# Gate tiles 4 and 5 of the second merge gate as a sixth pair by seven block products, and three convolution channels between the attention heads

## Chip, cores and metric

One core of a Trainium2 chip runs the whole program. The metric is device time in microseconds (us). The kernel before has a median of 817.81 us over 3 runs (817.81 to 818.59). Engines are named as in the profile: PE is the matmul engine, DVE the vector engine, ACT the scalar engine, POOL is GpSimd, and SP issues most of the loads.

## What is computed

The reference is one decoder layer on x of 512 tokens and 1024 channels, all in float32 (biases, gains and the second half are cut):

```python
u = _rmsnorm(h, norm1_g)
a_glu, q, k, v, r, g_low, gate_a, gate_b = _split_cols(u @ w_in)
c = a_glu[..., :CONV_CH] * jax.nn.sigmoid(a_glu[..., CONV_CH:])
c = _causal_dwconv(c, conv_dw_w, conv_dw_b)          # 31 taps over the tokens
y_conv = jax.nn.silu(_layernorm(c, ...)) @ w_conv_out
o = _gla_chunked(q, k, v, decay(g_low))               # 4 heads, chunks of 64 tokens
y_gla = (rmsnorm_by_head(o) * jax.nn.silu(r)) @ w_gla_out
merged = jax.nn.sigmoid(gate_a) * y_conv + jax.nn.sigmoid(gate_b) * y_gla
h = h + merged @ w_o
h = h + feed_forward(rmsnorm(h))
```

## The kernel before

**A tile of work.** Every projection is made in tiles of 128 output channels by 512 tokens; the 1024 input channels are eight blocks of 128. A float32 product is three matmuls in a rounded format (L529, L530, L531 in mm3): the weights and the activations are each split into a high part and a low rest, and the product of the two rests is left out. A plain tile is so 8 blocks by 3, 24 matmuls of 128x512. The names wlo and whi in the profile are the low and high part of a weight tile.

**Weights.** The list `order` (L244 to L274) fixes in which order weight tiles are loaded, split and used. ACT writes the high part (L414, L444), and the low part comes from one of three places: a subtraction on DVE (L415, L452), one on POOL (L450), or, for the tiles in the set ADDED, a negation on ACT (L446) and a DMA that adds the weights on top (L447). LOOK makes the split run two tiles ahead of its use. PE takes its weights strictly in that order, so a low part that comes late stops it.

**Seven products instead of eight.** Two kinds of work are done by a scheme of seven block products in place of eight on a 2 by 2 block matrix. In `seven` (L1440) w_r runs so, over all its tiles. In `two_tiles` (L1331) two gate tiles p and q are one pair: in four steps, x1, x3, x2 and x4, seven products of 128x256 matmuls, four input blocks by three each, which makes 84 matmuls. The sums of weights that a pair needs are made on POOL (L386), and the pair's results are put together by ACT copies (L1338) and DVE additions (L1341). The activations' own sums (L1293, L1306) are made once for w_r and all pairs. MERGE lists the pairs, `pair_7` (L1566) runs one of them, and BEHIND and PLAIN_GLA say which tiles of the w_gla and w_conv projections run inside a pair, by halves of four blocks, or behind it. Inside the first pair `pair_7` also runs `gated_o` (L1233), which transposes the gated head outputs on PE (L1237), two of them behind the last step of w_r already.

**The convolution.** Each of 8 channel tiles k has a gated unit (`glu`, L960), two weight tiles, from whose product the convolution's input comes. Its 31 taps are then worked off on the vector engines: `conv_chain` (L873) splits the tokens into even and odd, so that some 45 half-length taps do it. A tap is one DVE instruction (L889) of up to 255 elements, into the tiles called c and aside. A number of rows of taps per channel (ROWS) can go to POOL instead: ACT scales two tap inputs (L922) and one POOL addition of both halves (L924) stands for two DVE taps; `run_ahead` gives POOL these rows only while an earlier chain is being worked off, and those that it has not got to by then are DVE's. The list of one channel is the chain of that channel. `fill` (L505) hands out chain work by shares: each call of `weight` pays some work behind the DVE operation of the weight just split. The eight channels are then summed (L983, L986) for a normalization, whose statistics are spread on PE (L1014).

**The order of the stages.** w_v first half; channels 0 to 5 of the gated units; w_low; w_v second half; then a loop over the heads that overlaps queries and keys of one head (L1160 to L1173), and scores (L1188), states (L1199 to L1206) and outputs (L1217, L1219) of the head before; between these stand the late channels 6 and 7 (LATE_GLU, heads 1 and 2) and gate_b tiles 0 to 5 (AHEAD; heads 3 and the pass behind the last head); w_r; the five pairs with the w_gla tiles; w_conv; w_o; the feed-forward part. `pair_7(0)` works off every chain but the last of the list behind its third step (`while len(after) > 1`).

## Time and profile before

| what | value |
|---|---|
| time, median of 3 runs | 817.81 us |
| span of the profiled execution, first to last instruction | 816.3 us |
| median less span | 1.5 us |
| mean granted PE clock | 0.998 |
| w_low to the end of w_v | 98 to 124 us |
| heads and gate_b tiles | 124.6 to 246 us |
| w_r | 246 to 284.5 us |
| first pair, with two w_gla tiles behind it | 285.2 to 309.4 us |

The profiled execution has no time of its own beside its span; the 1.5 us are what lies around it, if it ran as the median did. The times of the stages are those of PE's rows in the trace. A row of the timeline gives start, duration, engine, line, operation, result and operands, a count where equal rows are joined, and in brackets the idle time of that engine before it with what ended it. A row of the windows gives for each engine the busy time in a stretch.

### The profile page before, as it was taken

What the parts mean: (1) busy time and instruction counts of PE and PEld (TensorE: products, weight loads), DVE (VectorE), ACT (ScalarE), POOL (GpSimd) and SP (SyncE); (2) the same over time, 40 slices, a digit from 0 to 9 for tenths busy, and PEclk for the clock granted to TensorE, in tenths of its full rate; (3) what the DMA queues carried; (4) which work ended last, traced back from release to release, by engine and by line L of the source; (5) the groups of instructions that cost most, each with busy time, mean ns of one, the idle gap of its engine ahead of it and who ended that gap; (6) DMA issues with size and microseconds to landing.
All of it is one profiled execution on the core that took longest, in us unless ns stands there. A gap on an engine that the chain in (4) does not pass through costs nothing.

```text
span 816.3 us, 11459 instructions
## 1 busy us (share of the span) xinstructions
PE 807.2 (99%) x4227; PEld 694.4 (85%) x4227; DVE 699.1 (86%) x1103; ACT 489.3 (60%) x749; POOL 192.6 (24%) x168
## 2 busy tenths in 40 slices
PE   9999999999999999999999999999999999999996
PEld 7888888888888898989888898898889987899885
DVE  6779999998998988486779899979976999789896
ACT  6667788677546665494535655556445663366555
POOL 2025433332204332122001100320123311622010
PEclk9999999999999999999999999999999999999999
DMA  9487758645831232432458513145732346224562
GB/s 338 143 196 181 189 160 177 160 116 133 189 97 58 80 128 78 142 108 89 166 136 217 176 64 118 52 155 155 160 120 82 142 116 167 104 104 173 163 129 104
DMA packets 36472, 113.60 MB, mean 139 GB/s; under 512 B 3688, under 2 KB 8944, under 8 KB 36416
## 3 DMA queue, kind: packets, MB, share of 16 engines
q1 hardware_dynamic: 28912, 86.39, 29.9%
q0 software_dynamic: 7488, 26.48, 18.1%
q8 instruction: 33, 0.54, 0.2%
q14 instruction: 23, 0.19, 0.1%
q10 hardware_dynamic: 16, 0.00, 0.0%
HBM read 110.76 MB, written 2.10 MB: 138 GB/s over the span
## 4 chain that ended last, share of the span: by engine, by line
PE 87%; DVE 11%; DMA 1%; issue 0%; ACT 0%; SPq 0%; ACTq 0%; DVEq 0%
PE mm L529 20%; PE mm L530 20%; PE mm L531 20%; DVE c L889 5%; PE cv L529 4%; PE cv L530 4%; PE cv L531 4%; DVE aside L889 3%; PE ax L531 2%; PE ax L530 2%; PE ax L529 2%; PE mm L743 2%; PE ax L1217 1%; PE cv L743 1%; PE ax L1219 1%; DMA raw<-in_w_v_dram 1%
## 5 line engine op out<-in xcount | busy, mean ns | idle before, releaser
L529 PE MATMUL mm<-uh,wlo 128*128 128x512 f32 (+1 forms) x532 | 194.2, 365 | 0.0
L530 PE MATMUL mm<-ul,whi 128*128 128x512 f32 (+1 forms) x532 | 191.9, 361 | 0.0
L531 PE MATMUL mm<-uh,whi 128*128 128x512 f32 (+1 forms) x532 | 191.7, 360 | 0.0
L415 DVE TENSOR_TENSOR wlo<-raw,whi 128x1024 fp32r<-128x1024 f32 x82 | 94.6, 1161 | 35.6 <-ACT whi L414 31.7
L386 POOL TENSOR_TENSOR raw<-raw,raw 128x512 f32<-128x512 f32 x39 | 61.8, 1585 | 235.6 <-DVE wlo L415 132.0
L529 PEld LDWEIGHTS mm<-uh,wlo 128*128 128x128 f32 x532 | 100.6, 189 | 15.2 <-DVE wlo L452 0.3
L531 PEld LDWEIGHTS mm<-uh,whi 128*128 128x128 f32 x532 | 100.5, 189 | 15.3
L530 PEld LDWEIGHTS mm<-ul,whi 128*128 128x128 f32 x532 | 100.6, 189 | 14.8
L414 ACT CAST whi<-raw 128x1024 fp32r<-128x1024 f32 x82 | 78.8, 965 | 40.0 <-PE mm L531 25.0
L444 ACT CAST whi<-raw 128x1024 fp32r<-128x1024 f32 x80 | 83.5, 1048 | 29.1 <-PE mm L531 13.9
L452 DVE TENSOR_TENSOR wlo<-raw,whi 128x1024 fp32r<-128x1024 f32 x50 | 66.0, 1326 | 7.2 <-ACT whi L444 7.0
L414 ACT CAST whi<-kept 128x1024 fp32r<-128x1024 f32 (+1 forms) x40 | 40.2, 1008 | 31.0 <-DVE kept L362 15.7
L415 DVE TENSOR_TENSOR wlo<-kept,whi 128x1024 fp32r<-128x1024 f32 (+1 forms) x40 | 47.4, 1186 | 6.4 <-ACT whi L414 6.4
L889 DVE SCALAR_TENSOR_TENSOR aside<-cv,pp,aside 128x255 f32<-128x255 f32 (+6 forms) x112 | 52.2, 466 | 0.0
L889 DVE SCALAR_TENSOR_TENSOR c<-aside,btmp,c 128x247 f32<-128x247 f32 (+13 forms) x93 | 52.0, 565 | 0.0
L889 DVE SCALAR_TENSOR_TENSOR c<-cv,pp,c 128x247 f32<-128x247 f32 (+13 forms) x93 | 43.3, 465 | 1.4 <-ACT c L885 1.4
L446 ACT ACTIVATE wlo<-raw 128x1024 fp32r<-128x1024 f32 x28 | 29.4, 1059 | 19.0 <-PE mm L529 19.0
L1338 ACT COPY tmp<-mm 128x256 f32<-128x256 f32 x38 | 14.1, 370 | 36.5 <-PE mm L531 35.8
L1720 DVE SCALAR_TENSOR_TENSOR tmp<-mm,pp,tmp 128x511 f32<-128x511 f32 (+1 forms) x42 | 31.2, 742 | 4.0 <-ACT tmp L1717 3.9
L1720 DVE SCALAR_TENSOR_TENSOR tmp<-tmp,pp,tmp 128x511 f32<-128x511 f32 (+1 forms) x32 | 27.8, 888 | 0.4
L1491 DVE TENSOR_TENSOR hres<-hres,mm 128x512 f32<-128x512 f32 (+1 forms) x37 | 24.6, 675 | 2.2 <-PE mm L531 2.1
L530 PE MATMUL cv<-ul,whi 128*128 128x512 f32 (+1 forms) x72 | 25.7, 356 | 0.0
(507 smaller groups left out, 2084.0 us busy)
## 6 DMA issues: line engine op xcount, KB each, us to landing
raw<-in_w_up_dram SPq DMA_DIRECT2D x44, 512.0 KB, 3.6
raw<-in_w_glu_dram SPq DMA_DIRECT2D x16, 512.0 KB, 5.7
raw<-in_w_down_dram SPq DMA_DIRECT2D x15, 512.0 KB, 3.3
wlo<-in_w_glu_dram POOLq DMA_DIRECT2D x12, 512.0 KB, 7.4
kept<-in_w_down_dram POOLq DMA_DIRECT2D x10, 512.0 KB, 5.5
raw<-in_w_v_dram SPq DMA_DIRECT2D x8, 512.0 KB, 6.4
raw<-in_w_qk_dram SPq DMA_DIRECT2D x8, 512.0 KB, 6.3
raw<-in_w_gb_dram SPq DMA_DIRECT2D x8, 512.0 KB, 4.0
```

The costliest lines, as they stand in the source:

```text
L386: work = nc.gpsimd.tensor_tensor(out, x, y, ALU.add)
L414: nc.scalar.copy(hi, raw)
L415: two_low[:] = [nc.vector.tensor_tensor(lo, raw, hi.bitcast(F32), ALU.subtract)]
L444: nc.scalar.copy(hi, raw)
L446: pace[0] = nc.scalar.mul(lo, raw, -1.0)
L452: pace[0] = nc.vector.tensor_tensor(lo, raw, hi.bitcast(F32), ALU.subtract)
L529: nc.tensor.matmul(acc, ll, rh, start=first, stop=False, **kw)
L530: nc.tensor.matmul(acc, lh, rl, start=False, stop=False, **kw)
L531: nc.tensor.matmul(acc, lh, rh, start=False, stop=last, **kw)
L889: nc.vector.scalar_tensor_tensor(out[:, j:], x[:, : half_t - j], w, out[:, j:], ALU.mult, ALU.add)
L1491: done = nc.vector.tensor_tensor(hres[t, n][:, c], hres[t, n][:, c], acc[:, c], op)
L1720: nc.vector.scalar_tensor_tensor(z[:, s:], acc[:, : T - s], w[j], z[:, s:], ALU.mult, ALU.add)
```

## The change

AHEAD goes from 6 to 4: gate_b tiles 4 and 5 are no longer plain tiles between the heads but the second of six pairs. LATE_GLU goes from 2 to 3: channel 5 of the gated units leaves the stretch before the heads, and channels 5, 6 and 7 come at heads 1, 2 and 3. The four gate_b tiles that stay plain all come in the pass behind the last head. w_gla tiles 2 to 7, not 2 to 5, run as halves inside pairs (the second, third and fourth). The rest shifts indices, and the shares that `fill` gets at gate_b tiles.

```diff
@@ -32,16 +32,16 @@
 EPS = 1e-6
 O_PAIRS = ((0, 2), (1, 3), (4, 6), (5, 7))
 GROUPS = (((0, 2), (1, 3), (4, 6), (5, 7)), ((8, 10), (9, 11), (20, 21)), ((12, 14), (13, 15), (16, 18), (17, 19)))
-AHEAD = 6
-
-MERGE = [("w_gb", 6, 7), ("w_ga", 0, 1), ("w_ga", 2, 3), ("w_ga", 4, 5), ("w_ga", 6, 7)]
+AHEAD = 4
+
+MERGE = [("w_gb", 6, 7), ("w_gb", 4, 5), ("w_ga", 0, 1), ("w_ga", 2, 3), ("w_ga", 4, 5), ("w_ga", 6, 7)]
 R_PAIRS = ((0, 4), (1, 5), (2, 6), (3, 7))
-LATE_GLU = 2
-_HALVES = [("w_gla", 2 + h // 2, h % 2) for h in range(8)]
-BEHIND = [[], _HALVES[:4], _HALVES[4:8]]
+LATE_GLU = 3
+_HALVES = [("w_gla", 2 + h // 2, h % 2) for h in range(12)]
+BEHIND = [[], _HALVES[:4], _HALVES[4:8], _HALVES[8:]]
 BEHIND += [[("w_conv", m, half) for m in pair for half in range(2)] for pair in O_PAIRS[:2]]
 MERGE_REST = [("w_conv", m) for pair in O_PAIRS[2:] for m in pair]
-PLAIN_GLA = {0: (0, 1), 2: (6, 7)}
+PLAIN_GLA = {0: (0, 1)}
 LOOK = 2
 
 ADDED = {("w_glu", j) for j in range(4, 2 * KT)} | {("w_qk", m) for m in range(KT)}
@@ -476,8 +476,8 @@
         quiet[0] = name == "w_v"
         if name == "w_qk":
             share = 1.0 if j < 2 else RATE
-        if name == "w_gb" and j > 3:
-            share = 2.0 if j == 4 else 6.8
+        if name == "w_gb" and j > 1:
+            share = 2.0 if j == 2 else 6.8
 
         fill(share + (1.75 if order[min(len(ready), len(order)) - 1] in ADDED else 0))
         return ready[used[0] - 1]
@@ -1397,17 +1397,17 @@
             new.decays()
             new.queries()
         else:
-            gate_b(2)
+            gate_b(0)
         if old:
             old.scores()
         if not new:
             urgent += n3_s1 + of_s1 + of_n2
-        new.keys() if new else gate_b(3)
+        new.keys() if new else gate_b(1)
         if old:
             old.states()
-            next(late_glu) if h <= LATE_GLU else gate_b(0 if new else 4)
+            next(late_glu) if h <= LATE_GLU else gate_b(2)
             old.outputs()
-            next(late_glu) if h <= LATE_GLU else gate_b(1 if new else 5)
+            next(late_glu) if h <= LATE_GLU else gate_b(3)
     behind += [roots_at[0]]
     gla_scope.close()
     late_scope, late = scoped("late", 1, "right")
@@ -1581,7 +1581,7 @@
                     gated_o(m, ax_bank)
                 if j == 2:
                     start_norms()
-            if j == 0 or n >= 2:
+            if j == 0 or n >= 3:
 
                 while complete_pairs:
                     complete_pairs.pop(0)()
@@ -1593,7 +1593,7 @@
                         (part if name == "w_gb" else gas)[m] = sigmoid(m, c)
 
                 complete_pairs.append(sigmoids)
-                if n >= 2:
+                if n >= 3:
                     complete_pairs.pop()()
             for proj, m, half in behind[j : j + 1]:
                 open_tiles[proj, m] = tile_of(proj, m, half_of[half], open_tiles.get((proj, m)))
@@ -1609,7 +1609,7 @@
         hold.clear()
         start_chain()
 
-    for n in range(3):
+    for n in range(4):
         pair_7(n)
         for m in PLAIN_GLA.get(n, ()):
             tile_of("w_gla", m, range(KT))
@@ -1618,7 +1618,7 @@
         if m not in merged_tiles:
             j = [m in p for p in O_PAIRS].index(True)
             if j < 2:
-                pair_7(3 + j)
+                pair_7(4 + j)
             else:
                 tile_of("w_conv", m, range(KT))
         return merged_tiles[m]
```

PE has 4059 rows in place of 4023, 36 more: 84 matmuls of 128x256 for 48 of 128x512. DVE has 29 more: 22 taps (298 L889 become 320), 4 of L415, 3 of L1341. POOL has 11 fewer L924 (27 become 16), 2 fewer L447 and 4 more L386; ACT has 22 fewer L922, 2 fewer each of L444 and L446, 4 more each of L414 and L1338, and 2 more table loads.

**POOL, in the head loop.** wlo are the low parts that the DMAs make up, c the convolution channels, rstd a root for the head norm. Before:

```order
L581 TENSOR_TENSOR rstd_252_1615<-mean_251_1613,mhalf_92 128x4
L924 TENSOR_TENSOR c_270_1688<-c_270_1688,btmp_89_434 128x2x248
L924 TENSOR_TENSOR c_270_1688<-c_270_1688,tmp_90_435 128x2x249
L447 DMA wlo_278_1754<-in_w_glu_dram 128x1024
L924 TENSOR_TENSOR c_270_1688<-c_270_1688,btmp_89_434 128x2x250
L447 DMA wlo_288_1816<-in_w_qk_dram 128x1024
L447 DMA wlo_302_1887<-in_w_qk_dram 128x1024
L447 DMA wlo_312_1943<-in_w_gb_dram 128x1024
L581 TENSOR_TENSOR rstd_300_1880<-mean_299_1878,mhalf_92 128x4
L924 TENSOR_TENSOR c_314_1951<-c_314_1951,btmp_89_434 128x2x248
L924 TENSOR_TENSOR c_314_1951<-c_314_1951,tmp_90_435 128x2x249
```

And now, from the last channel weights to the last but one gate_b tile:

```order
L447 DMA wlo_256_1567<-in_w_glu_dram 128x1024
L581 TENSOR_TENSOR rstd_240_1499<-mean_239_1497,mhalf_92 128x4
L447 DMA wlo_266_1633<-in_w_glu_dram 128x1024
L447 DMA wlo_276_1691<-in_w_qk_dram 128x1024
L447 DMA wlo_290_1762<-in_w_qk_dram 128x1024
L447 DMA wlo_300_1819<-in_w_glu_dram 128x1024
L581 TENSOR_TENSOR rstd_288_1755<-mean_287_1753,mhalf_92 128x4
L447 DMA wlo_310_1885<-in_w_glu_dram 128x1024
L447 DMA wlo_320_1943<-in_w_gb_dram 128x1024
```

The POOL additions of the last three channels (L924; before 8, 3 and 2 for channels 5, 6 and 7) are gone; their taps stand on DVE.

**DVE, at the end of w_r.** wlo are w_r's low parts here, r and h the gate r and the head outputs that it multiplies, kept the sums of w_r's weights, c and aside the last channel of the convolution. Before, the last two w_r weights and what lies around them:

```order
L415 TENSOR_TENSOR wlo_447_2621<-raw_394_2371,whi_446_2620 128x1024
L1541 TENSOR_TENSOR r_442_2600<-mm_407_2429,r_442_2600 128x512
L1548 TENSOR_TENSOR h_254_1619<-h_254_1619,r_420_2477 128x512
L415 TENSOR_TENSOR wlo_449_2656<-kept_333_2078,whi_448_2655 128x1024
L1541 TENSOR_TENSOR r_443_2614<-mm_408_2430,r_443_2614 128x512
L1548 TENSOR_TENSOR h_345_2140<-h_345_2140,r_442_2600 128x512
L415 TENSOR_TENSOR wlo_453_2665<-kept_351_2153,whi_452_2664 128x1024
L1541 TENSOR_TENSOR r_434_2560<-r_434_2560,cv_405_2427 128x512
```

The same stretch now, up to the last w_r weights (wlo_442 is what wlo_453 was):

```order
L415 TENSOR_TENSOR wlo_436_2514<-raw_383_2247,whi_435_2513 128x1024
L889 SCALAR_TENSOR_TENSOR aside_88_433<-cv_345_2071,pp_89,aside_88_433 128x246
L889 SCALAR_TENSOR_TENSOR c_346_2074<-cv_345_2071,pp_89,c_346_2074 128x245
L889 SCALAR_TENSOR_TENSOR aside_88_433<-cv_345_2071,pp_89,aside_88_433 128x245
L1541 TENSOR_TENSOR r_431_2489<-mm_396_2306,r_431_2489 128x512
L1548 TENSOR_TENSOR h_242_1503<-h_242_1503,r_411_2360 128x512
L1541 TENSOR_TENSOR r_432_2503<-mm_397_2307,r_432_2503 128x512
L415 TENSOR_TENSOR wlo_438_2552<-kept_321_1947,whi_437_2551 128x1024
L1548 TENSOR_TENSOR h_333_2009<-h_333_2009,r_431_2489 128x512
L889 SCALAR_TENSOR_TENSOR c_346_2074<-cv_345_2071,pp_89,c_346_2074 128x244
L889 SCALAR_TENSOR_TENSOR aside_88_433<-cv_345_2071,pp_89,aside_88_433 128x244
L415 TENSOR_TENSOR wlo_442_2564<-kept_339_2022,whi_441_2563 128x1024
```

Before, the last channel's chain was over ahead of w_r; now its taps stand between w_r's weights: 23 of them between the second w_r weights and the first weights of the first pair, 5 more up to the last of the four head outputs that the first pair transposes. The low parts of the first pair's x1 and x3 weights now also stand ahead of that output, and behind it before.

**PE, at the start of the first pair.** ax are the banks of the transposes, h the gated head outputs of four token tiles, mm the pair's sum; wlo and whi with 128x256 are the pair's first weights. Before, eight transposes stood in a block ahead of the pair:

```order
L531 MATMUL mm_406_2428<-whi_452_2664,uh_4_99 128x512
L1237 MATMUL ax_460_2738<-ident_84,h_345_2140 128x128
L1237 MATMUL ax_460_2738<-ident_84,h_346_2142 128x128
L1237 MATMUL ax_460_2738<-ident_84,h_347_2144 128x128
L1237 MATMUL ax_460_2738<-ident_84,h_348_2146 128x128
L1237 MATMUL ax_463_2747<-ident_84,h_345_2140 128x128
L1237 MATMUL ax_463_2747<-ident_84,h_346_2142 128x128
L1237 MATMUL ax_463_2747<-ident_84,h_347_2144 128x128
L1237 MATMUL ax_463_2747<-ident_84,h_348_2146 128x128
L529 MATMUL mm_467_2760<-uh_2_97,wlo_455_2699 128x256
```

Now the two of the first output stand some 25 rows earlier, between the last matmuls of w_r, and four stand ahead of the pair:

```order
L531 MATMUL mm_395_2305<-whi_441_2563,uh_4_99 128x512
L1237 MATMUL ax_449_2647<-ident_84,h_334_2011 128x128
L1237 MATMUL ax_449_2647<-ident_84,h_335_2013 128x128
L1237 MATMUL ax_452_2656<-ident_84,h_334_2011 128x128
L1237 MATMUL ax_452_2656<-ident_84,h_335_2013 128x128
L529 MATMUL mm_456_2669<-uh_2_97,wlo_444_2602 128x256
```

and the two of the last output inside the pair's first product:

```order
L529 MATMUL mm_456_2669<-uh_2_97,wlo_444_2602 128x256
L530 MATMUL mm_456_2669<-ul_3_98,whi_443_2601 128x256
L1237 MATMUL ax_449_2647<-ident_84,h_336_2015 128x128
L1237 MATMUL ax_452_2656<-ident_84,h_336_2015 128x128
L531 MATMUL mm_456_2669<-uh_2_97,whi_443_2601 128x256
```

The transposes now wait in the middle of a product, eight matmuls into the pair, for the last output.

## The prediction

> **What bounds the kernel now.** I read the page's engine rows first, then the windows by stage, and then the timeline of PE and DVE around w_r and the first pair.
>
> ```profile
> span 816.3 us, 11459 instructions
> ...
> PE 807.2 (99%) x4227; PEld 694.4 (85%) x4227; DVE 699.1 (86%) x1103; ACT 489.3 (60%) x749; POOL 192.6 (24%) x168
> ...
> DVE  6779999998998988486779899979976999789896
> ```
>
> PE is the bound: 807.2 of 816.3 us. DVE stands at 86%, but its slices are at eight or nine tenths for much of the first third, so the windows of the heads (the first four) and of w_r (the last) come next.
>
> ```profile
> 126.00:158.00 32.00, 31.87 (x145) 25.95 (x144) 32.00 (x68) 24.30 (x41) 14.97 (x14) 1.00 0.77 175
> 158.00:186.00 28.00, 28.00 (x131) 23.54 (x131) 27.96 (x65) 20.24 (x38) 8.29 (x8) 1.00 0.52 125
> 186.00:214.00 28.00, 27.98 (x131) 23.13 (x129) 24.59 (x62) 19.81 (x37) 7.25 (x7) 1.00 0.64 150
> 214.00:242.00 28.00, 28.00 (x131) 23.55 (x130) 27.97 (x53) 13.99 (x33) 1.95 (x2) 1.00 0.41 100
> 242.00:285.00 43.00, 43.00 (x193) 35.39 (x193) 37.32 (x39) 26.97 (x40) 15.64 (x9) 1.00 0.25 86
> ```
>
> The columns are the length, then busy time of PE, PE's loads, DVE, ACT and POOL. PE loses 0.15 us in 159 us, and DVE is full in three of the five windows. There are two nearly full engines here: PE sets the time only as long as DVE's backlog is worked off before PE asks for what stands behind it. Any DVE work that is added or made later, and any PE time that is taken out ahead of it, is measured against that.
>
> **What PE gains.** Rows of PE at the start of one plain tile and of the next, and at the start and end of the first step of the second pair:
>
> ```profile
> 87.47 0.39 PE L529 MATMUL mm<-uh,wlo 128*128 128x512 f32 x1
> ...
> 92.91 0.39 PE L529 MATMUL mm<-uh,wlo 128*128 128x512 f32 x1
> ...
> 309.35 0.28 PE L529 MATMUL mm<-uh,wlo 128*128 128x256 f32 x1
> ...
> 312.23 0.40 PE L529 MATMUL mm<-oa,wlo 128*128 128x512 f32 x1
> ```
>
> A plain tile of 24 matmuls takes 92.91 − 87.47 = 5.44 us, 0.2267 each; 24 of 128x256 take 312.23 − 309.35 = 2.88, 0.120 each, which is more than half. Two plain gate tiles are 10.88 us, a pair of 84 is 84 × 0.120 = 10.08. PE gains 0.80 us, a tenth of a per cent. The w_gla tiles that move into pairs keep their count and shape: nothing.
>
> [...]
>
> **What moves.** Channel 5's two tiles, 10.88 us, leave the stretch before the heads, so PE reaches everything from w_low to w_r 10.88 us earlier; the pair pays 10.08 back behind the first pair. What matters is the last channel. Before, its value was there when DVE's L967 ran; its chain was done, and the last of the channel sums with it, long before w_r:
>
> ```profile
> 194.60 0.69 DVE L967 TENSOR_TENSOR h<-mm,tmp 128x512 f32<-128x512 f32 x1
> ...
> 225.65 0.69 DVE L986 TENSOR_TENSOR btmp<-btmp,c 128x512 f32<-128x512 f32 x1
> ```
>
> ```profile
> 218.77 0.39 PE L529 MATMUL mm<-uh,wlo 128*128 128x512 f32 x1
> ```
>
> ```profile
> 246.16 0.39 PE L529 MATMUL cv<-whi,ul 128*128 128x512 f32 x1
> ```
>
> The last channel now takes the places of gate_b tiles 0 and 1, the second of which ended at 218.77. Less 10.88 that is 207.9, and w_r begins at 246.16 − 10.88 = 235.3. Before, the channel had 246.2 − 194.6 = 51.6 us ahead of w_r; it now has 27.4, in which DVE also finishes channel 6 and makes the activation sums. The taps that find no place stand between w_r's weights in the new order: 23 between the second w_r weights and the first pair's, 28 up to the last of the outputs that the pair transposes.
>
> **How much DVE work.** Groups of taps, one of the groups on POOL, and a few rows where both run:
>
> ```profile
> L889 DVE SCALAR_TENSOR_TENSOR c<-aside,btmp,c 128x247 f32<-128x247 f32 (+13 forms) x93 | 52.0, 565 | 0.0
> L889 DVE SCALAR_TENSOR_TENSOR c<-cv,pp,c 128x247 f32<-128x247 f32 (+13 forms) x93 | 43.3, 465 | 1.4 <-ACT c L885 1.4
> ```
>
> ```profile
> L924 POOL TENSOR_TENSOR c<-c,tmp 128x502 f32<-128x502 f32 (+3 forms) x14 | 17.6, 1254 | 8.2 <-ACT tmp L922 7.4
> ```
>
> ```profile
> 69.09 0.48 DVE L889 SCALAR_TENSOR_TENSOR c<-aside,btmp,c 128x255 f32<-128x255 f32 x1
> 69.48 0.48 DVE L889 SCALAR_TENSOR_TENSOR aside<-cv,pp,aside 128x255 f32<-128x255 f32 x1
> 69.88 1.45 DVE L889 SCALAR_TENSOR_TENSOR c<-aside,btmp,c 128x250 f32<-128x250 f32 x1
> ```
>
> ```profile
> 69.78 1.26 POOL L924 TENSOR_TENSOR c<-c,tmp 128x502 f32<-128x502 f32 x1 [0.63 <-ACT tmp L922]
> ```
>
> An undisturbed tap is issued every 69.48 − 69.09 = 0.39 us. Eleven POOL additions become 22 taps: + 22 × 0.39 = 8.6 us of DVE. Against it stands that a tap with two operands from the main memory (aside, btmp) is stretched while POOL adds: 0.48 us becomes 1.45, and over all 93 of them the mean is 565 − 465 = 100 ns above the other kind, 9.3 us for 27 additions or 0.34 for one. Eleven fewer give back 3.8 us by that mean, and 11 × 0.97 = 10.7 if each saved a whole stretch like the one at 69.88. So DVE's load grows by 4.8 us, bounds − 2.1 and + 8.6, and PE asks 10.88 us earlier. In the heads I cost it at nothing: DVE's idle 0.04 + 3.41 + 0.03 us there is little, but what is pushed back there is the chain and not PE's operands, since the weights of the channels, heads and gate_b tiles come from ACT and DMA. That cover ends with w_r, whose low parts DVE makes itself in turn with the taps.
>
> **The sum at w_r.** DVE's waits, its disturbed rows, and the two handovers, before:
>
> ```profile
> 249.36 0.96 DVE L1306 TENSOR_TENSOR hq<-hq,sumsq 128x512 fp32r<-128x512 f32 x1 [3.04 <-ACT sumsq L1301]
> 250.80 1.23 DVE L415 TENSOR_TENSOR wlo<-raw,whi 128x1024 fp32r<-128x1024 f32 x1 [0.48 <-ACT whi L414]
> 252.23 1.23 DVE L415 TENSOR_TENSOR wlo<-kept,whi 128x1024 fp32r<-128x1024 f32 x1 [0.21 <-ACT whi L414]
> ...
> 256.37 1.72 DVE L362 TENSOR_TENSOR kept<-kept,raw 128x1024 f32<-128x1024 f32 x1
> ...
> 267.89 1.23 DVE L415 TENSOR_TENSOR wlo<-raw,whi 128x1024 fp32r<-128x1024 f32 x1 [1.02 <-ACT whi L414]
> 269.69 1.22 DVE L415 TENSOR_TENSOR wlo<-raw,whi 128x1024 fp32r<-128x1024 f32 x1 [0.58 <-ACT whi L414]
> ...
> 271.44 1.64 DVE L1548 TENSOR_TENSOR h<-h,r 128x512 f32<-128x512 f32 x1
> 273.34 1.98 DVE L415 TENSOR_TENSOR wlo<-kept,whi 128x1024 fp32r<-128x1024 f32 x1 [0.26 <-ACT whi L414]
> ...
> 279.88 0.68 DVE L1548 TENSOR_TENSOR h<-h,r 128x512 f32<-128x512 f32 x1
> 280.48 2.35 DVE L415 TENSOR_TENSOR wlo<-raw,whi 128x1024 fp32r<-128x1024 f32 x2
> ```
>
> ```profile
> 253.18 0.39 PE L530 MATMUL ax<-wlo,uh 128*128 128x512 f32 x1
> ```
>
> ```profile
> 284.45 1.03 PE L1237 MATMUL ax<-ident,h 128*128 128x128 f32 x8
> ...
> 285.24 0.36 PE L529 MATMUL mm<-uh,wlo 128*128 128x256 f32 x1
> ```
>
> The second w_r weights end at 250.80 + 1.23 = 252.03, 1.15 ahead of their use. From there to the pair DVE waits 0.21 + 1.02 + 0.58 + 0.26 = 2.07 us, all for ACT, and taps can fill that. The pair's first weights end at 281.7 (half of the 2.35 behind 280.48), 3.5 ahead of 285.24. With 23 taps: 23 × 0.39 − 2.07 − 3.5 = 3.4 us late. The last gated output ends at 279.88 + 0.68 = 280.56; the fourth transpose begins some 0.3 behind 284.45, 4.2 later. It now has 28 taps and the pair's two low parts (2.35) ahead of it, and its transposes stand eight matmuls (0.96) into the pair: 28 × 0.39 + 2.35 − 2.07 − 4.2 − 0.96 = 6.0 us late. That is PE's whole loss, since the 3.4 are part of it. Downwards: the taps ahead of the second weights (6, or 2.3 us) fill the waits of 3.04 + 0.48 there, and if ACT allows, the lead grows by 3.52 − 2.34 = 1.2; and the rows at 256.37, 271.44 and 273.34 are stretched by POOL by 0.5, 1.0 and 0.8 against equal rows (1.22, 0.68, 1.22), 2.3 us that taps with a PSUM operand would not suffer. So 2.5 to 6.0. I take the middle, 4.2, since neither end has a row that decides it. Weights further on have their lead from this stall: a lost microsecond of PE is a gained one for DVE. The new pair's other costs, 4 POOL sums, 4 copies and 3 additions, lie in pairs where DVE and ACT have room (in the last window DVE leaves 5.7 of 43 us, POOL 27): nothing; without that cover, 4 sums of 1.6 us.
>
> The sum: − 0.8 + 4.2 = + 3.4 us. Against the profiled 816.3 that is 819.7, and with the 1.5 us around the span, as for the median of 817.81, **821.2**.
>
> **Rivals.** First, DVE catches up. For it speaks that most of the POOL additions on which DVE's slowest taps fall are gone ahead of w_r; if each saved a stretch of 0.97, DVE's load falls by 2.1 us, the chain comes to w_r some 7 us (4.8 + 2.1) further on than I assume, 18 taps fewer are left there, and the loss is 0 to 1. Against it speaks that the mean, 0.34, is a third of that, and the chain cannot start before 207.9. The time: − 0.8 to + 0.2, so 817.0 to 818.0, not slower. It decides from some 15 taps fewer in w_r. [...]
>
> Second, the lateness is larger: contention moves onto the taps in w_r, half of which read aside and btmp, while POOL makes w_r's and the pair's weight sums; with 3 of them stretched by 0.97 and the ACT waits not filled (2.07), the loss is 6.0 + 2.9 + 2.1 = 11 at most, about 8 likely: 825.
>
> Third, it is faster. The 0.8 and all that PE waits for weights (the window of 126 to 158 loses 0.13, and the list of waits has the row below) make 1.3 us at most, 816.5; beyond 0.2% it would need a gain that no row shows.
>
> ```profile
> PE mm L529 <- ACT whi L444: 0.4, 1, 0.4
> ```
>
> That the pair is not made is no case: PE's rows are 36 more, as 84 − 48.
>
> **Chances and range.** What a measurement of this kernel can tell from no change is about 0.2%, 1.6 us: faster is below 816.2, slower above 819.4. The forecast, 818.0 to 823.0 (a loss of 1 to 6), has 0.58; its part below 819.4 some 0.10. DVE catching up has 0.24, the larger lateness 0.11, the gain beyond 816.2 0.07. So faster 0.07, same 0.34, slower 0.59. The range takes in the forecast's bounds and the first rival and stops within the second: 816.8 to 824.0.
>
> **What would show it.** Right: PE idle of 2 to 6 us between the end of w_r and the first product of the first pair, released by DVE (L415 or L1548), DVE at 100% from 208 us to there, taps of L889 between its L415 rows, and 10.08 us for the second pair. Wrong: PE at the first pair without a gap and DVE waiting for ACT in w_r as before (first rival); or PE's gaps spread over w_r and the heads, with DVE's taps at 0.7 us and more (second).

## The result and the profile after

| | before | changed |
|---|---|---|
| median | 818.2 us | 826.56 us |
| runs | 817.81 to 818.92 | 825.34 to 828.08 |
| span of the profiled run | 816.3 us | 823.6 us |

The changed kernel takes 1.0103 times the time of before (95% interval 1.0091 to 1.0114), 8.4 us more at the medians and 7.3 in the profiled spans. The direction was forecast, the size was not: 821.2 was predicted, and 824.0 was the end of the range.

The engine rows of the page of the changed kernel:

```profile
span 823.6 us, 11529 instructions
...
PE 808.2 (98%) x4263; PEld 696.6 (85%) x4263; DVE 712.5 (87%) x1132; ACT 483.4 (59%) x733; POOL 186.5 (23%) x159
```

PE is still the bound, but it now stands still somewhere. (The pages count 4227 rows of PE before and 4263 now; the 4023 and 4059 given ahead of the prediction count fewer, with the same difference of 36.) The list of PE's waits says for whom (us in total, number of waits, longest):

```profile
PE mm L529 <- DVE r L1541: 2.8, 1, 2.8
PE mm L529 <- DVE h L1084: 2.1, 1, 2.1
PE mm L649 <- DVE ones L622: 1.1, 1, 1.1
PE ax L1237 <- DVE h L1548: 1.1, 1, 1.1
PE mm L743 <- ACT h L670: 0.7, 1, 0.7
PE mm L530 <- DVE wlo L415: 0.5, 1, 0.5
PE mm L529 <- DVE hres L1491: 0.5, 1, 0.5
```

Two of these (L649 and L743) are at the start of the run and were there before. The other five are all on DVE. The last (L1491) comes late, at 607 us, where the kernel before had its 0.4 us for L444 at 693 us instead. In the timeline of PE the other four stand at two places, one behind w_low and three in w_r; below them are the rows behind the longest:

```profile
98.69 0.50 PE L529 MATMUL mm<-whi,ul 128*128 128x512 f32 x1 [2.08 <-DVE h L1084]
...
253.71 0.50 PE L530 MATMUL mm<-wlo,hq 128*128 128x512 f32 x1 [0.53 <-DVE wlo L415]
...
271.24 0.55 PE L1237 MATMUL ax<-ident,h 128*128 128x128 f32 x3 [1.08 <-DVE h L1548]
...
274.58 0.77 PE L529 MATMUL mm<-whi,ul 128*128 128x512 f32 x1 [2.79 <-DVE r L1541]
275.14 0.63 PE L530 MATMUL mm<-wlo,uh 128*128 128x512 f32 x1
275.57 0.63 PE L531 MATMUL mm<-whi,uh 128*128 128x512 f32 x1
...
277.70 0.46 PE L530 MATMUL mm<-wlo,uh 128*128 128x512 f32 x1
```

Matmuls behind the wait of 2.79 us are issued every 0.43 us, not 0.227: 277.70 − 274.58 = 3.12 us for seven of them, 1.53 more than 7 × 0.227. The windows (length; busy us of PE, PE's loads, DVE, ACT, POOL; granted clock; DMA) show the granted clock there, and DVE in the stretch that the prediction showed before:

```profile
274.50:277.00 2.50, 2.42 (x6) 1.97 (x7) 2.50 (x4) 1.23 (x2) 0.00 (x0) 0.50 0.03 7
242.00:285.00 43.00, 38.60 (x177) 31.52 (x176) 42.38 (x61) 22.95 (x30) 9.54 (x6) 0.96 0.18 62
```

DVE has 42.38 of 43 us of work where it had 37.32, and the granted clock of PE is half for 3.41 us, from 274.41 to 277.83. The pair itself costs what was worked out. Its rows, from the first to the last of its seven products, with halves of w_gla tiles between them:

```profile
306.22 0.28 PE L529 MATMUL mm<-uh,wlo 128*128 128x256 f32 x1
...
309.10 0.40 PE L529 MATMUL mm<-oa,wlo 128*128 128x512 f32 x1
...
311.84 0.28 PE L529 MATMUL mm<-hq,wlo 128*128 128x256 f32 x1
...
314.72 0.40 PE L529 MATMUL mm<-h,wlo 128*128 128x512 f32 x1
...
317.46 0.28 PE L529 MATMUL mm<-sumsq,wlo 128*128 128x256 f32 x1
...
320.34 0.40 PE L529 MATMUL cv<-oa,wlo 128*128 128x512 f32 x1
...
323.08 0.28 PE L529 MATMUL mm<-uh,wlo 128*128 128x256 f32 x1
...
324.52 0.40 PE L529 MATMUL cv<-h,wlo 128*128 128x512 f32 x1
```

2.88 + 2.88 + 2.88 + 1.44 = 10.08 us, for two plain tiles of 10.88. So the account of the span closes: − 0.80 for the pair, + 2.08 behind w_low, + 0.53 + 1.08 + 2.79 = 4.40 of waits in w_r, + 1.53 of lower clock make 7.21 us, of 7.3 measured. That it closes to a tenth is partly luck. PE's first row of w_r comes 9.7 us earlier than before (236.47 and 246.16 us), where 10.88 − 2.08 would be 8.8, and from there to the first pair it takes 45.5 us in place of 39.1, 6.4 more and not 5.93. These smaller differences, which are not explained, nearly cancel.

### The profile page after: what moved, and what is told of

It reads as the page before. It is cut to its first block, busy times and chain, and to the rows that moved or that the text cites. A ratio compares the mean times of both kernels' runs of the same rounds, so it can differ in the third digit from the quotient of the medians.

```text
span 823.6 us, 11529 instructions
## 1 busy us (share of the span) xinstructions
PE 808.2 (98%) x4263; PEld 696.6 (85%) x4263; DVE 712.5 (87%) x1132; ACT 483.4 (59%) x733; POOL 186.5 (23%) x159
## 4 chain that ended last, share of the span: by engine, by line
PE 86%; DVE 9%; DMA 3%; ACT 1%; issue 1%; POOL 0%; SPq 0%; ACTq 0%
PE mm L529 20%; PE mm L530 20%; PE mm L531 20%; PE cv L529 4%; PE cv L530 4%; PE cv L531 4%; DVE wlo L415 2%; PE ax L531 2%; PE ax L529 2%; PE ax L530 2%; PE mm L743 2%; DMA kept<-in_w_down_dram 2%; DVE c L889 1%; DMA raw<-in_w_v_dram 1%; DVE aside L889 1%; DVE kept L362 1%
## 5 line engine op out<-in xcount | busy, mean ns | idle before, releaser
L529 PE MATMUL mm<-uh,wlo 128*128 128x512 f32 (+1 forms) x528 | 190.9, 362 | 0.0
L530 PE MATMUL mm<-ul,whi 128*128 128x512 f32 (+1 forms) x528 | 188.7, 357 | 0.0
L531 PE MATMUL mm<-uh,whi 128*128 128x512 f32 (+1 forms) x528 | 188.6, 357 | 0.0
L415 DVE TENSOR_TENSOR wlo<-raw,whi 128x1024 fp32r<-128x1024 f32 x86 | 104.1, 1216 | 31.3 <-ACT whi L414 27.4
L386 POOL TENSOR_TENSOR raw<-raw,raw 128x512 f32<-128x512 f32 x42 | 68.1, 1622 | 240.7 <-DVE wlo L415 133.3
L414 ACT CAST whi<-raw 128x1024 fp32r<-128x1024 f32 x86 | 82.6, 963 | 38.3 <-PE mm L531 18.1
L444 ACT CAST whi<-raw 128x1024 fp32r<-128x1024 f32 x78 | 81.2, 1046 | 31.1 <-PE mm L531 16.1
L452 DVE TENSOR_TENSOR wlo<-raw,whi 128x1024 fp32r<-128x1024 f32 x50 | 65.5, 1315 | 7.1 <-ACT whi L444 7.0
L414 ACT CAST whi<-kept 128x1024 fp32r<-128x1024 f32 (+1 forms) x40 | 40.2, 1007 | 40.0 <-DVE kept L362 19.4
L889 DVE SCALAR_TENSOR_TENSOR c<-aside,btmp,c 128x249 f32<-128x249 f32 (+14 forms) x104 | 54.1, 528 | 1.5 <-ACT c L885 1.4
L889 DVE SCALAR_TENSOR_TENSOR aside<-cv,pp,aside 128x255 f32<-128x255 f32 (+6 forms) x112 | 52.4, 468 | 2.3 <-ACT cv L880 2.3
L415 DVE TENSOR_TENSOR wlo<-kept,whi 128x1024 fp32r<-128x1024 f32 (+1 forms) x40 | 46.5, 1165 | 7.7 <-ACT whi L414 7.6
L889 DVE SCALAR_TENSOR_TENSOR c<-cv,pp,c 128x249 f32<-128x249 f32 (+14 forms) x104 | 48.6, 467 | 2.5 <-ACT c L885 2.5
L446 ACT ACTIVATE wlo<-raw 128x1024 fp32r<-128x1024 f32 x26 | 27.3, 1058 | 33.1 <-PE mm L529 28.4
L1338 ACT COPY tmp<-mm 128x256 f32<-128x256 f32 x45 | 16.5, 368 | 34.6 <-PE mm L531 34.2
L1491 DVE TENSOR_TENSOR hres<-hres,mm 128x512 f32<-128x512 f32 (+1 forms) x37 | 24.6, 674 | 3.5 <-PE mm L531 2.2
L386 POOL TENSOR_TENSOR raw<-raw 128x512 f32<-128x512 f32 x14 | 26.3, 1878 | 0.0
```

What stands on the lines that cost most here:

```text
L386: work = nc.gpsimd.tensor_tensor(out, x, y, ALU.add)
L414: nc.scalar.copy(hi, raw)
L415: two_low[:] = [nc.vector.tensor_tensor(lo, raw, hi.bitcast(F32), ALU.subtract)]
L444: nc.scalar.copy(hi, raw)
L446: pace[0] = nc.scalar.mul(lo, raw, -1.0)
L452: pace[0] = nc.vector.tensor_tensor(lo, raw, hi.bitcast(F32), ALU.subtract)
```

## The experiments

The theory after the result was the one of the prediction, with w_low added: the late channel's taps stand between w_r's weights and make DVE late. Its rival: PE now comes to w_r 10.9 us earlier, and DVE is late for that alone, taps or no taps. Spans of profiled runs are compared with 816.3 us of before, medians with the before of the same chip.

**e1: the pair without the third late channel.**

```diff
-LATE_GLU = 3
+LATE_GLU = 2
...
-        else:
-            gate_b(0)
...
-        new.keys() if new else gate_b(1)
+        new.keys() if new else gate_b(2)
...
             old.states()
-            next(late_glu) if h <= LATE_GLU else gate_b(2)
+            next(late_glu) if h <= LATE_GLU else gate_b(0 if new else 3)
             old.outputs()
-            next(late_glu) if h <= LATE_GLU else gate_b(3)
+            if h <= LATE_GLU:
+                next(late_glu)
+            elif new:
+                gate_b(1)
```

> The sixth pair without the third late channel: LATE_GLU stays 2, gate_b tiles 0 and 1 stay at head 3, tiles 2 and 3 come around the last head's states, and channel 5 stays ahead of the heads. Theory (the late channel makes DVE late, the pair itself pays): no wait at w_low, no wait and no lower clock in w_r, and the pair's 0.8 us: about 817.4 us, ratio to before 0.999. Rival (two gate tiles fewer ahead of w_r bring PE to it 10.9 us earlier, and that alone makes DVE late there): a gap of 2 to 4 us in w_r as in the changed kernel, 820 us or more.

Measured: 826.85 us (before 817.92), ratio 1.0107 (1.0092 to 1.0122). The wait behind w_low is gone, but w_r loses as much as in the changed kernel, though only 3 taps stand behind the first of the activation sums here, and 1 of them in w_r. Its PE waits:

```profile
221.02 1.16 PE L1188 MATMUL ax<-q,k 128*128 128x128 f32 x8 [1.56 <-ACT h L1229]
...
250.35 0.50 PE L530 MATMUL mm<-wlo,c 128*128 128x512 f32 x1 [1.77 <-DVE wlo L415]
...
276.39 0.47 PE L529 MATMUL mm<-whi,ul 128*128 128x512 f32 x1 [2.60 <-DVE r L1542]
```

The first belongs to the new order alone: no tile stands ahead of the last head's scores. The other two, 4.4 us, are those of w_r. The theory fell and the rival held: taking two plain tiles from ahead of w_r is enough. Not all of it is the amount of DVE's work, though. Just ahead of the first of the two waits DVE itself stood idle for ACT, as it did before (3.04 us); from there on it is busy without a pause up to the second (the window has its length, then busy us of PE, PE's loads, DVE, ACT, POOL):

```profile
245.41 1.70 DVE L1306 TENSOR_TENSOR sumsq<-tmpq,sumsq 128x512 fp32r<-128x512 f32 x1 [2.52 <-ACT sumsq L1301]
```

```profile
250.00:276.50 26.50, 23.55 (x96) 18.91 (x97) 26.50 (x30) 13.29 (x18) 5.55 (x3) 0.94 0.17 59
```

So the second wait, 2.60 us, is DVE's backlog, and the first, 1.77, is in part a handover.

**e2: three late channels without the pair.**

```diff
-LATE_GLU = 2
+LATE_GLU = 3
...
+    gate_b(4)
+    gate_b(5)
```

> Three late channels without the sixth pair: LATE_GLU 3, AHEAD stays 6, all six plain gate_b tiles behind the last head's queries. Theory: the wait at w_low stays (2.1 us), while w_r comes 10.9 us later than in the changed kernel, so that its waits (4.4 us) and the lower clock (1.6 us) go: about 820.5 us. Rival (the order of taps between w_r's weights makes the loss wherever PE stands): 4.4 + 1.6 + 2.1 us as in the changed kernel, about 826.

Measured: 823.2 us, ratio 1.0065 (1.0043 to 1.0088), with some spread (821.43 to 824.98), between the 820.5 of the theory and the 826 of its rival. In the profile, which is of the fastest run, PE waits 2.58 us behind w_low, and 0.41 and 0.93 in w_r. Of the 36 taps behind the first of the activation sums only 6 still run in w_r, against 30 in the changed kernel, since PE comes there 11.7 us later (248.16 and 236.47 us), and w_r loses 1.3 us and not 6. So each half of the change loses by itself, at different places, and the two halves are not a sum: + 8.9 and + 5.3 us alone, + 8.4 together.

**e3: the taps moved out of w_r.**

```diff
-        share = {"two": 2.5, "w_glu": RATE, "w_r": 2.0}.get(name, RATE)
+        share = {"two": 2.5, "w_glu": RATE, "w_r": 0.5}.get(name, RATE)
...
-            if n == 0 and j == 2:
+            if n == 1 and j == 2:
                 while len(after) > 1:
                     fill(1)
+                start_norms()
...
-                if j == 2:
-                    start_norms()
```

> The changed kernel with the share at w_r's weights 0.5 in place of 2.0, and the last chain finished inside the second pair and not the first: 9 taps in place of 37 ahead of the first pair's sums. Theory: w_r loses nothing and keeps its clock, w_low's 2.1 us stay: 826.6 - 4.4 - 1.6 = 820.6 us. Rival (the backlog only moves on and stops PE in the second pair): 824 us or more, with PE waits for L415 or L1341 from 300 to 325 us.

Measured: 832.33 us, ratio 1.0177 (1.0162 to 1.0192). The waits in w_r went down to 0.65 and 0.29 us, as expected, but the backlog came due elsewhere: the first tile behind the pair is given the PSUM bank (one of the tiles mm, ax and cv, into which PE's rows write) from which the last channel's taps still read.

```profile
302.50 0.79 PE L529 MATMUL cv<-oa,wlo 128*128 128x512 f32 x1 [3.52 <-DVE c L889]
```

```profile
100.07:103.48 3.41, 3.41 (x10) 2.62 (x9) 3.41 (x9) 2.56 (x4) 1.44 (x2) 0.50 0.04 16
...
304.87:308.29 3.42, 3.42 (x14) 3.03 (x13) 3.42 (x7) 0.00 (x0) 1.21 (x1) 0.50 0.33 116
```

Around the 3.52 us the clock is half, from 301.46 to 308.29 us, some 3 us lost (half of the 5.79 from 302.50 on). It was half behind w_low too, where PE waited 2.33 us, some 1.7 us lost (half of 3.41) that the changed kernel did not lose. The norm of the convolution is late as well (waits of 0.2 to 0.6 us from 380 us on, 1.7 together). The rival of the expectation held, with another waiter than it named.

**e4: matmuls in the gap.**

```diff
+                if (name, step, i) == ("w_r", "a22", 0):
+                    for _ in range(10):
+                        ah, w_ = acts[0][step][0][:, :P], parts[0][1][0][:, :T]
+                        nc.tensor.matmul(bank["z"][0], ah, w_, start=True, stop=True)
                 products(step, i, parts, acc)
```

> The changed kernel with ten further 128x512 matmuls, whose result nobody reads, ahead of w_r's last step, where PE stood still for 2.8 us. Theory (the lower clock behind the gap costs 1.6 us of its own): the gap is filled with 2.3 us of work, the granted clock stays 1.00 from 275 to 279 us, about 825.0 us. Rival (the clock costs nothing that the late DVE would not cost anyway): 826.6 us.

Measured: 827.28 us, ratio 1.0119 (1.0102 to 1.0135). The granted clock stays at 1.00 from 242 to 290 us, and yet nothing is gained: PE still waits 2.12 us at w_r's last step, and now 1.00 us at the last output's transposes inside the first pair, where the changed kernel, at its lower clock, did not wait. The lower clock in w_r is therefore no price of its own; PE slowed down while it would have waited for DVE.

**e5: half of the time given back ahead of w_r.**

```diff
+    spare = ax_bank()
+    for _ in range(24):
+        nc.tensor.matmul(spare, acts1[0][0][:, :P], acts1[0][0], start=True, stop=True)
     seven("w_r", R_PAIRS, [ByTile(k) for k in range(4)], None, r_at, put=put_r, before=sums_for)
```

> The changed kernel with 24 further 128x512 matmuls (5.44 us, nobody reads them) ahead of w_r, half of the time by which the two gate_b tiles moved behind it. Theory (DVE has a fixed amount of work ahead of the end of w_r, and PE waits there for whatever it arrives early): the dummies take the place of the waits and of the lower clock, about 826.5 us as without them. Rival (the waits belong to the order of taps and weights in w_r): 826.6 + 5.4 = 832 us.

Measured: 828.5 us (824.66 to 829.81), ratio 1.0115 (1.0087 to 1.0143). In the profiled run one wait of 0.57 us is left in w_r of 4.40, and the clock there is 1.00. But w_r begins 9.5 us later than in the changed kernel (246.00 and 236.47 us), and only 5.44 of that is the useless work. The rest was lost behind w_low, where this run's wait was longer than in the changed kernel and the clock was half for 6.83 us, from 98.90 to 105.73:

```profile
100.19 0.80 PE L529 MATMUL mm<-whi,ul 128*128 128x512 f32 x1 [3.26 <-DVE h L1084]
```

So this is no clean half of the shift. The median lies above the theory's 826.5, but the interval ends at 818.17 × 1.0143 = 829.9, below the rival's 832, and the waits show the exchange: PE waits in w_r for what it came early.

**e6: the last channel's taps left out.** Of that channel only the first taps are made, 44 DVE taps fewer, so its output is not the reference's.

```diff
-            return (0.6, lambda: part(i, j))
+            return (0.6, lambda: part(i, j) if k < KT - 1 else None)
```

> The changed kernel without the taps of the last channel but its first ones (left out: 44 DVE taps, 17 us of DVE; that channel of the convolution is wrong). Theory (backlog of DVE): nothing to wait for in w_r, w_low's 2.1 us stay: 826.6 - 6.0 = 820.6 us. Rival (what is late are the handovers between ACT, POOL and DVE around the head norm and w_r's sums, which also made the pair alone wait): 824 us or more.

Measured: 820.25 us, ratio 1.003 (1.0017 to 1.0043); the waits are 2.44 behind w_low and 0.29 in w_r. With 17 us less for DVE, w_r loses nothing, although DVE still stands idle for 3.03 us for ACT's sums (L1301) at its start. So the handovers alone do not make PE wait, and as the order of the taps fell in e1, the amount of DVE work is left.

**e7 and e8: less work handed out at w_low, and a later flush.** e7:

```diff
+        if name == "w_low":
+            share = -1.75
```

> The changed kernel with no chain work handed out at w_low's two weight tiles, so that 7 rows fewer stand ahead of L1084 on DVE; the chains then overlap otherwise, and POOL gets 27 rows of taps as before (DVE 22 taps fewer than in the changed kernel). Theory: the 2.1 us at w_low go, and w_r loses less by the 22 taps less 11 stretches (8.6 - 3.8 = 4.8 us): 819.5 to 821 us. Rival for w_low (it is the handover of the conv bank, an idle 2.3 us of DVE, that makes L1084 late): the wait stays, 822 us or more.

Measured: 829.97 us, ratio 1.0147 (1.0128 to 1.0167). The 819.5 to 821 of the theory did not come. L1084 comes earlier, but PE still waits 1.52 for it, and w_r loses more: 1.45 (for ACT), 1.02 and 3.92 us (for DVE), with the clock at half for 10.2 us in all. DVE has 22 taps fewer to do, yet 40 in place of 37 were left behind the first of the activation sums. The stretch from 110 to 215 us, first in the changed kernel, then in e7:

```profile
110.00:215.00 105.00, 105.00 (x486) 87.92 (x485) 102.20 (x243) 71.92 (x125) 25.01 (x25) 1.00 0.68 160
```

```profile
110.00:215.00 105.00, 105.00 (x487) 87.97 (x486) 90.13 (x217) 79.31 (x146) 37.73 (x36) 1.00 0.68 156
```

DVE was busy for 90.1 us there and not for 102.2. Of these 12.1 us the 22 taps that POOL took over are 8.6, but DVE also stood still for 12.6 us, in two waits for POOL's additions of a chain, of which this is the first:

```profile
168.19 0.48 DVE L891 SCALAR_TENSOR_TENSOR c<-cv,pp,c 128x253 f32<-128x253 f32 x1 [6.32 <-POOL c L926]
```

What it did not do in the heads it owed in w_r.

e8 adds e3's shares and flush, and keeps that PSUM bank from being lent:

```diff
-                bank_turns.extend(["mm"] * 4 + ["cv"])
+                bank_turns.extend(["mm"] * 40 + ["cv"])
```

> As e7, and with the share at w_r's weights 0.5, the last chain finished inside the second pair, and the convolution's PSUM bank not lent out to tiles while that chain still reads it. Theory: no wait at w_low, w_r or for the bank, the pair's gain of 0.8 us is seen: 817.1 us. Rival (the norm of the convolution then comes late, as in e3 at 380 us, or the lump of taps stops PE in the second pair): 820 us or more.

Measured: 834.25 us, ratio 1.0197 (1.0175 to 1.022). The 817.1 of the theory did not come either. There is no wait for the bank, and w_r has 1.8 us left, but now the flush stops PE in the second pair for 5.13 us (a low part, L415), and w_low has 2.69. Where the backlog is put, there PE waits.

**e9 and e10: another bank for w_low's result.**

```diff
-    plow = mm_bank()
+    plow = ax_bank()
```

> The changed kernel with w_low's result in a bank of the ax group and not of the mm group, so that w_v's second half does not wait for L1084 on DVE. Theory (DVE has a fixed amount of work up to the end of w_r): PE comes to w_r some 2.1 us earlier and waits there as much longer, about 826.5 us, with 8 us lost in w_r in place of 6. Rival (the two places are apart and add up): 826.6 - 2.1 = 824.5 us.

> As e9, and without the taps of the last channel but its first ones (left out as in e6). With the backlog and the wait both gone, what is left is the arithmetic of PE: 818.2 - 0.8 = 817.4 us and no wait of PE over 0.3 us in the first 430 us. If the pair's 84 matmuls cost more than 10.1 us: over 818.2 us.

Measured: e9 828.15 us, ratio 1.0116 (1.0102 to 1.013); e10, with e6's taps left out as well, 821.48, ratio 1.0031 (1.0019 to 1.0043). The edit missed: the bank is free, but the next row of PE reads L1084's result and waits for it, 1.25 us in e9 and 2.73 in e10. Neither tells the theories apart.

**e11: the changed kernel once more,** as the measure for these.

> The changed kernel once more, as the measure for the two others on the same chip: 826.6 us, with about 2 us of wait at w_low and 6 us of waits and lower clock in w_r; if the wait at w_low passes 3 us, a lower clock there too and up to 829 us.

Measured: 827.05 us (825.63 to 828.92), ratio 1.011 (1.0095 to 1.0124), with 2.22 behind w_low and 0.65, 1.08 and 2.79 in w_r. The 3 us at which the expectation puts a lower clock behind w_low are an estimate; of the runs before, e5 (3.26 us), e8 (2.69) and e3 (2.33) had one there, and this run had none (1.00 from 80 to 110 us).

**e12 and e13: L1084 taken off DVE.**

```diff
-    nc.vector.tensor_tensor(glow[rows], plow[rows], glow[rows].bitcast(F32), ALU.subtract)
+    kept_low = tmp()
+    nc.scalar.copy(kept_low[rows], plow[rows])
+    nc.gpsimd.tensor_tensor(glow[rows], kept_low[rows], glow[rows].bitcast(F32), ALU.subtract)
```

> The changed kernel with the low rest of w_low's result made by an ACT copy and a POOL subtraction in place of L1084 on DVE, so that nothing at w_low waits for DVE. Theory (a fixed amount of DVE work up to the end of w_r): the 2.1 us at w_low go and come back in w_r, whose waits and lower clock grow from 6 to about 8 us: 826.5 to 827 us. Rival (the two add up): w_r stays at 6 us, 824.7 us.

> As e12, and without the taps of the last channel but its first ones (left out). With neither wait, what is left is PE's own work: 818.3 - 0.8 = 817.5 us, and no PE wait over 0.5 us between 20 and 430 us. If the sixth pair costs more than its 10.1 us on PE: over 818.3 us.

Measured: e12 827.67 us, ratio 1.0111 (1.0098 to 1.0125); e13, with e6's taps left out, 820.11, ratio 1.0021 (1.0012 to 1.003). PE's waits of over 0.3 us in e12 between 20 and 430 us:

```profile
94.20 0.50 PE L529 MATMUL mm<-whi,ul 128*128 128x512 f32 x1 [0.77 <-ACT tmp L1085]
...
133.42 0.55 PE L1181 MATMUL ax<-ident,k 128*128 128x128 f32 x3 [1.35 <-DVE k L1175]
255.54 0.50 PE L530 MATMUL mm<-wlo,hq 128*128 128x512 f32 x1 [1.27 <-DVE wlo L415]
273.07 0.55 PE L1239 MATMUL ax<-ident,h 128*128 128x128 f32 x3 [1.12 <-DVE h L1550]
276.41 0.77 PE L529 MATMUL mm<-whi,ul 128*128 128x512 f32 x1 [2.79 <-DVE r L1543]
```

Of 2.08 us behind w_low 0.77 is left, and the rest came back: 1.35 in the first head, 5.2 of waits in w_r in place of 4.40, and the clock at half there for 6.83 us in place of 3.41. The rival's 824.7 did not come: what is saved at w_low is waited for later. It came back with more than 1.3 us, though. Why DVE is late in the first head (1.35) is not shown; what differs around the same wait of 2.79 us, behind which the lower clock lasts twice as long, is in the last section. The theory of a fixed amount of work gives the direction here, not the size. In e13 PE's waits between 20 and 430 us are 0.72, 0.32, 1.37 and 0.28, together 2.69, and less the pair's 0.80 that is 1.89, for a span that is 818.2 − 816.3 = 1.9 longer. The expected 817.5 did not come, because these waits stayed; apart from them the pair gains its 0.8 us, as its rows have it, and no more.

What stays open: the price of the lower clock by itself. It falls into time in which DVE is late, and e4 shows that in w_r it costs nothing; behind w_low and in e3, it may be a real loss, but no run took it away there. No version was found that beats before: what there is to win is 0.8 us, less than a measurement here can tell.

## Why the prediction was wrong

**The gain.** Right: 0.80 us was worked out, and the pair's rows give 10.08 us.

**"In the heads I cost it at nothing."** This is the step that failed first: all that PE reaches earlier ahead of w_r was put at nothing, and it cost 2.08 us. The reason given, that PE's operands there come from ACT and DMA, holds for weights and not for L1084, the low rest of w_low's result, which stands ahead of the heads and which DVE makes in turn with the taps. Before, it had little to spare, by the rows of DVE and of the PE matmul that needs its bank (the second of two):

```profile
105.93 0.70 DVE L1084 TENSOR_TENSOR h<-mm,h 16x512 fp32r<-16x512 f32 x1
```

```profile
106.74 0.62 PE L529 MATMUL mm<-whi,ul 128*128 128x512 f32 x2
```

The result is there at 105.93 + 0.70 = 106.63, and the second of the two joined matmuls begins at some 106.97, a third of a microsecond later. With channel 5's tiles gone from ahead of it, it was 2.08 us late. Every result that DVE makes for PE should have had its spare time read, not only the low parts.

**The sum at w_r, 4.2 us.** Mis-sized, at its upper bound: 4.40 of waits and 1.53 of lower clock, 5.9, where 2.5 to 6.0 stood. The middle was taken because no row decided; the lower end rested on two reliefs, that the taps fill ACT's waits and that POOL's stretches fall away. The first came, but gave less: DVE has no idle time left in w_r (45.53 of 45.53 us, 33.40 of 39.08 before), and the second weights, done at 239.42 + 2.31 = 241.73, lead their use at 243.50 by 1.8 us in place of 1.15, a gain of 0.6 where 1.2 was hoped for. The second did not come, as the rows at 238 to 251 us show:

```profile
237.98 1.52 DVE L889 SCALAR_TENSOR_TENSOR c<-aside,btmp,c 128x254 f32<-128x254 f32 x1
239.42 2.31 DVE L415 TENSOR_TENSOR wlo<-raw,whi 128x1024 fp32r<-128x1024 f32 x1
...
247.25 4.07 DVE L362 TENSOR_TENSOR kept<-kept,raw 128x1024 f32<-128x1024 f32 x2
```

POOL's weight sums (L373, from 237.36 to 240.64 and from 246.70 to 250.24 us) still fall on DVE rows with two operands (0.47 us undisturbed at 242.04, 1.21 at 255.10, twice that for two): 3.8 us in these three, where the three rows before had 2.3. Over the whole run the taps (L889) keep DVE busy for 135.35 us in place of 128.03, 7.3 more, where 4.8 was put and 8.6 was the bound: the POOL additions that went gave back little. No term of the sum had the clock.

**Where PE waits there.** Half right: the waits are on DVE, but the gap between the end of w_r and the first pair, which was named as the sign, did not come. The low parts and the outputs were followed, but not the PSUM bank: the longest wait, 2.79 us, is w_r's last step waiting until L1541 has read the bank of the step before. The transposes inside the first pair, on which the 6.0 rested, did not wait, since PE had been stopped before them; in e4, where it was stopped less, they did, for 1.00 us.

**What made DVE late.** The prediction named the taps between the weights; e1 has one there and loses as much. The cause is the sum that the prediction began with and left: DVE has the same amount of work up to the first pair, within 1 us, and PE comes to w_r 9 to 10 us earlier for it. From the start of the run to the first row of the first pair, before, in the changed kernel and in e1:

```profile
0.00:285.24 285.24, 283.09 (x1292) 234.70 (x1292) 257.56 (x512) 199.62 (x329) 87.34 (x90) 1.00 0.59 158
0.00:282.00 282.00, 273.71 (x1243) 226.97 (x1243) 258.40 (x524) 185.65 (x300) 72.37 (x77) 0.99 0.58 153
0.00:282.71 282.71, 274.91 (x1243) 227.12 (x1244) 257.50 (x512) 194.74 (x323) 85.92 (x88) 0.99 0.58 152
```

DVE (the third number behind the length) is busy for 257.6, 258.4 and 257.5 us there, and PE, busy for 9.4 and 8.2 us less, gains only some 3 us of time. More time ahead of w_r (e5) or less work (e6) takes the waits away, and e12 fits in direction.

**The rivals.** The second, a larger lateness at 825 us with 0.11, came nearest with its number, and that is luck: not three more stretched taps and ACT's waits made it, but w_low and the clock. DVE did not catch up, and nothing was faster. In the profiled run w_low and the larger loss in w_r are 2.08 + 1.73 = 3.8 us of the 3.9 by which the span passes the 819.7 of the prediction. Most of the remaining 1.5 us at the median is that the profiled run was the fastest of four; the runs now spread from 825.3 to 828.1, before from 817.8 to 818.9, and the two slowest have the lowest mean clock (0.994 and 0.995, against 0.996).

## What to carry to other kernels

Moving work of the bounding engine behind a stage, even at a gain, brings that engine earlier to everything ahead, and an engine that is 86% busy on the average may have no room there: add up the second engine's work up to the stage's end against the time left, before looking at the order in detail. Then read the spare time of every handover to the bounding engine, its accumulator banks and small results too, and not only that of its operands. A wait that is taken away at one place while the second engine stays short comes back at the next, so only less work for it, or more time, counts.

## What the runs showed of the hardware

The granted clock of PE falls to half around some of its waits, and the length of the wait alone does not say around which: it did with 1.77 us in e1 and 2.33 us in e3, and did not with 2.44 us in e6 and 2.73 us in e10 (1.00 from 80 to 110 us in both) or with 2.60 us in e1. Behind such waits the half rate lasts 3.41 us or a multiple of it (6.83 us in e3, e5, e9 and e12, 10.24 in e8), and in two traces edges were seen to lie a whole multiple of 3.41 us apart: in e3 the clock comes back at 103.48 and falls again at 301.46 us, 58 times 3.413 later; in the changed kernel it comes back at 277.83 and falls at 820.54, behind the last matmul, 159 times 3.413 later. That this grid holds in the other traces is an assumption. On it, PE's busy time in a window (the first number behind the length) can be read against the clock (0.50 or 1.00). First the changed kernel, then e1, then e4 (whose next window, from 275.48, is at 1.00), then e12:

```profile
96.92:100.33 3.41, 1.64 (x7) 1.37 (x8) 3.35 (x9) 0.27 (x1) 0.00 (x0) 1.00 0.79 288
100.33:103.74 3.41, 3.41 (x17) 2.83 (x16) 3.41 (x8) 3.33 (x5) 2.22 (x2) 1.00 0.02 10
...
271.00:274.41 3.41, 0.55 (x3) 0.31 (x3) 3.41 (x8) 1.00 (x2) 0.00 (x0) 1.00 0.00 0
274.41:277.83 3.42, 3.25 (x8) 2.60 (x9) 3.42 (x7) 1.26 (x2) 0.00 (x0) 0.50 0.02 5
277.83:281.24 3.41, 3.41 (x17) 2.81 (x16) 3.41 (x5) 1.23 (x2) 1.30 (x1) 1.00 0.00 0
```

```profile
247.88:251.29 3.41, 1.64 (x8) 1.04 (x7) 3.41 (x5) 2.72 (x4) 0.39 (x1) 1.00 0.00 0
251.29:254.70 3.41, 3.41 (x10) 2.51 (x9) 3.41 (x4) 1.48 (x2) 0.00 (x0) 0.50 0.00 0
...
271.77:275.18 3.41, 2.02 (x9) 1.32 (x8) 3.41 (x4) 0.63 (x1) 0.46 (x1) 1.00 0.00 0
275.18:278.59 3.41, 2.20 (x10) 1.87 (x11) 3.41 (x6) 2.31 (x3) 0.00 (x0) 1.00 0.00 0
```

```profile
272.07:275.48 3.41, 1.68 (x8) 1.06 (x6) 3.41 (x7) 1.32 (x2) 0.00 (x0) 1.00 0.00 0
```

```profile
271.70:275.12 3.42, 0.80 (x5) 0.31 (x3) 3.42 (x6) 2.13 (x3) 0.00 (x0) 1.00 0.00 0
275.12:278.53 3.41, 2.12 (x5) 1.78 (x6) 3.41 (x7) 1.26 (x2) 0.00 (x0) 0.50 0.00 0
278.53:281.94 3.41, 3.41 (x9) 2.67 (x9) 3.41 (x7) 0.04 (x1) 0.32 (x1) 0.50 0.02 5
```

At full rate, the windows with 0.55 us of PE's work (the changed kernel), 0.80 (e12) and 1.64 (e1) are followed by the half rate; those with 1.68 (e4), 2.02 and 2.20 (e1), and with 1.64 in the changed kernel at 96.92, are not. So the same 1.64 us went both ways, and a limit was not shown. The 2.60 us of e1 lie over two of these windows, 1.39 and 1.21 us in each. At half rate, the window with 2.12 us of work (e12) is followed by half rate again, the one with 3.25 us (the changed kernel) by full. The same wait of 2.79 us came with 3.41 us of half clock in the changed kernel, where it ended 0.17 us behind an edge, and with 6.83 in e9 and e12, where 1.3 us of it lay behind the edge. Where the edges lie is the difference that these traces show; that it is the cause is the author's reading. The busy time is modelled, so these numbers are good to some hundredths at best.
